# All heads load their projections from pair results; plain gate blocks and the up-projections run as filler beside the attention

## The chip, the core and the metric

The kernel runs on one NeuronCore of one Trainium2 chip. The metric is the device time of one execution in microseconds. Engines: TensorE (PE) with its weight loads (PEld), VectorE (DVE), ScalarE (ACT), GpSimd (POOL), SyncE (SP, here the queue that issues most DMAs).

## What is computed

One layer of a streaming encoder for 512 prompt tokens and 8 x 16 sample tokens, 640 columns in all, D_MODEL 2048. One combined projection feeds three attention branches and three merge gates:

```
parts = rms_norm(x, g_pre) @ w_in      # 6 stick heads q,k,v,g | 6 band heads q,k,v,g | 4 memory heads q,g | 3 gates of 2048
o_sb  = stick_breaking(q, k, v)        # strictly causal, sigmoids and a running product
o_bd  = band_attention(q, k, v, bias)  # softmax over own chunk and the 8 before
o_mm  = memory_attention(q, mk, mv)    # softmax over 256 memory tokens
branch(o, g, w) = (o * silu(g)) @ w
merged = sigmoid(mg_sb) * branch(o_sb, sg, w_up_sb) + sigmoid(mg_bd) * branch(o_bd, bg, w_up_band) \
       + sigmoid(mg_mm) * branch(o_mm, mg, w_up_mem)
y = x + rms_norm(merged @ w_out, g_post)
```

The 128 sample rows attend to caches of 512 rows (256 for memory) for each of 8 streams. Keys and values of the new tokens are outputs too. All is float32.

## The kernel before, in words

A float32 product is made of three matmuls of rounded parts: `split` casts a source to `hi` on ACT and subtracts on DVE for `lo`; then hi x hi, hi x lo, lo x hi. Tokens stand in columns, 640 in two halves of 320. A block is 128 output columns of the combined projection: 16 row tiles x 3 x 2 halves = 96 matmuls. Weights come by SP in half blocks (`wr`, 3 buffers) and are split into `wh` and `wl`. There are 56 head blocks (24 for stick heads, 24 for band heads, 8 for memory heads) and 48 gate blocks.

The stages, in order of the trace:

- Memory keys and values, normalised `x`, and four plain gate blocks (`gate`, `x_proj`): to 137 us.
- Pairs (`block_pair`): two blocks at once with seven half-size products in place of eight, 168 matmuls. 12 pairs make all blocks of the band heads, whose raw results go to DRAM by POOL (`put_raw` into `raw_d`); 22 pairs make the other 44 gate blocks, whose sigmoids go to DRAM by ACT's queue (`put_gate` into `sig_d`). Beside them SP cuts the caches' keys into `keys_d`. To 975 us.
- Attention, 16 heads in the order of `ORDER` (0 to 5 stick, 6 to 11 band, 12 to 15 memory). Band heads load their four raw results (`loaded`, `head_g`); stick heads make their four blocks here and memory heads two, as plain blocks (`transposed`, `head_g`: L383, L393, L394). `head_g` drains its accumulator with a sigmoid on ACT and a multiplication on DVE into an `sg` tile of the pool `stg`, three buffers, which a head holds until its output is written to `osg_d`. A head has three generators: the prompt's attention (11 steps, 9 for memory heads), the samples' score (11 steps) and the samples' output (3 steps); `interleave` goes round them, with the output of the head before.
- Up-projections (`up`): three branches x 16 blocks. `load_o` reads `osg_d` and splits it into `oh` and `ol`; each block is multiplied by a gate from `sig_d` and added into `merged`. These tiles lie where `x` lay, so they wait for the last projection of `x`. To 1858 us.
- The output projection, norm and residual.

Accumulators for projections (`acc`) have two buffers of two PSUM banks; the attention shares four single banks. The program is written in the order of the code, but a planner orders each engine's queue when it is built, by dependencies and its own idea of durations. `tc.issue_after(ins)` binds it: what the block traces on the engine of `ins` comes after `ins` in that queue; it is no wait for its end. Before, only projections are bound so, each behind the one before (`last_mm`); the attention's matmuls stand wherever the planner puts them.

Of the kernel before, what the change touches and what calls it, by code (L numbers as in the profile page):

```python
# [36 lines left out]

FIRST = 4


ORDER = (0, 6, 1, 7, 12, 2, 8, 3, 9, 13, 4, 5, 14, 15, 10, 11)
# [5 lines left out]
def stream_step_kernel(  # L47
# [47 lines left out]
    raw_d = [[dpool.tile([P, NT], F32, name=f"raw_d{n}_{h}") for h in range(6)] for n in range(4)]  # L95
# [92 lines left out]

    def x_proj(col, acc):
# [181 lines left out]
    def loaded(n, h):  # L371
        t = pa.tile([P, NT], F32, tag=f"l{n}", name=f"l{n}", bufs=2 if n == 0 else 1)
# [3 lines left out]
    def transposed(col, n, raw):  # L376

        if raw is not None:
            return loaded(n, raw)
        acc = new_acc()  # L380
        x_proj(col, acc)
        t = pa.tile([P, NT], F32, tag=f"l{n}", name=f"l{n}", bufs=2 if n == 0 else 1)
        ACT.copy(halves(t), acc[:, :, :HF])  # L383
        return t

    def head_g(col, raw=None):
        sg = stg.tile([P, NT], F32, tag="sig", name="sg")
        if raw is not None:
            SP.dma_start(sg, raw_d[3][raw])
            return sg  # L390
        acc = new_acc()
        x_proj(col, acc)
        ACT.activation(halves(sg), acc[:, :, :HF], AF.Sigmoid)  # L393
        DVE.tensor_tensor(halves(sg), acc[:, :, :HF], halves(sg), op=ALU.mult)  # L394
        return sg
# [205 lines left out]
    def causal_head(i):  # L601

        kind, h, c0 = ("sb", i, C_SB) if i < 6 else ("bd", i - 6, C_BD)
# [15 lines left out]
        raw = h if kind == "bd" else None  # L619
        sg = head_g(c0 + 2304 + h * P, raw)  # L620
        vt = transposed(c0 + 1536 + h * P, 2, raw)
# [7 lines left out]
        qt = transposed(c0 + h * P, 0, raw)  # L629
        kt = transposed(c0 + 768 + h * P, 1, raw)  # L630
# [19 lines left out]
    def mem_head(h):  # L650
# [4 lines left out]
        qt = transposed(C_MM + h * P, 0, None)  # L655
        sg = head_g(C_MM + 512 + h * P)
# [26 lines left out]
    def gate(i):  # L683
        acc = new_acc()
        x_proj(C_GATE + i * P, acc)
# [29 lines left out]
    for i in range(FIRST):  # L715
        gate(i)
# [110 lines left out]
    pairs = [(C_BD + 768 * n + h * P, put_raw(n, h)) for n in range(4) for h in range(0, 6, 2)]  # L827
    pairs += [(C_GATE + i * P, put_gate(i)) for i in range(FIRST, 3 * KB, 2)]
# [10 lines left out]
    back = True  # L839
    with tc.tile_pool(name="att", bufs=1, reuse_waits="tile") as pa:  # L840
        qm, wTm = zero_padded(4)

        rest = iter(())
# [4 lines left out]
        interleave(rest)  # L848
    xs.close()

    br = ExitStack()
    pm = br.enter_context(tc.tile_pool(name="mraw", bufs=1, side="right", reuse_waits="tile"))
    merged = pm.tile([P, KB, NT], F32, name="merged")
    po = br.enter_context(tc.tile_pool(name="osgp", bufs=6, side="right", reuse_waits="tile"))
    branches = ((w_up_sb, 6, 0, 0), (w_up_mem, 4, 12, 2 * KB), (w_up_band, 6, 6, KB))
    parts, mark = {}, None

    def load_o(i):
        r = po.tile([P, NT], F32, tag="sig", name="or", bufs=5)
        SP.dma_start(r, osg_d[i])  # L860
        hh = po.tile([P, NT], F32R, tag="oh", name="oh")
        ll = po.tile([P, NT], F32R, tag="ol", name="ol")
        split(hh, ll, r)
        return hh, ll

    def o_src(k):
        return [[t[:, j * HF:(j + 1) * HF] for j in range(2)] for t in parts[k]]

    def up(i):
        nonlocal mark  # L870
        w_up, nh, i0, g0 = branches[i // KB]
        j = i % KB
        if j == 0:
            for h in range(nh):
                parts[h] = load_o(i0 + h)
                if i == 0:
                    mark = last_on(SP)
        acc = new_acc()
        with tc.issue_after(mark if i > 1 else last_mm):
            proj(w_up[0], j * P, nh, o_src, acc)  # L880
        sig = po.tile([P, NT], F32, tag="sig", name="sig", bufs=5)
        with tc.issue_after(mark):
            SP.dma_start(sig, sig_d[g0 + j])
        if i < KB:
            DVE.tensor_tensor(halves(merged[:, j]), acc[:, :, :HF], halves(sig), op=ALU.mult)
        else:
# [115 lines left out]
```

## Time and profile before

| | us |
|---|---|
| median of 3 runs (2084.43 to 2088.02) | 2087.05 |
| the profiled execution | 2088.03 |
| its span, first to last instruction | 2086.3 |
| PE busy | 2045.1 (98%) |
| DVE / ACT / POOL busy | 1104.4 / 817.0 / 570.1 |
| mean granted TensorE clock | 0.994 of 2.4 GHz |

The busy time of PE is made of matmuls whose ends are modelled, so a stretch can be busy and still not at its best pace; the pace is read from the starts. An idle engine costs only where the end of the program hangs on it. A line such as L115 is that of a helper (`split`) with many callers, so groups are told by their tiles.

### The profile page before, as it was taken

How to read it: one execution, taken by the hardware profiler on the slowest of the kernel's cores; microseconds unless marked ns; L12 is line 12 of the kernel's file. 1: busy time of each engine (PE TensorE's matmuls, PEld its weight loads, DVE VectorE, ACT ScalarE, POOL GpSimd, SP SyncE). 2: the span in 40 equal slices, each digit the busy share in tenths (PEclk: the TensorE clock that was granted, in tenths of full speed). 3: DMA queues.
4: the chain of work that ended last, by engine and by line, in shares of the span. 5: the costliest groups of instructions: out<-in, count | busy, mean ns of one | idle time of the engine just before them, and what ended most of it. 6: DMA issues, size and time to landing. Idle time of an engine off the chain costs nothing.

```text
span 2086.3 us, 35971 instructions
## 1 busy us (share of the span) xinstructions
PE 2045.1 (98%) x13997; PEld 1934.7 (93%) x13997; DVE 1104.4 (53%) x1804; ACT 817.0 (39%) x1567; POOL 570.1 (27%) x539
## 2 busy tenths in 40 slices
PE   7999999999999999999999999989999999999998
PEld 5999999999999999999999799979998899998886
DVE  6875555555555555555355645555455665542234
ACT  6543444444444444444233333333334232322221
POOL 1155455664444444441010101010100015330000
PEclk9999999999999999999999999989999999999999
DMA  7656665565556655645557646653556875532225
GB/s 264 213 145 157 166 162 146 140 154 147 147 138 162 164 140 136 154 127 167 154 157 214 186 131 197 195 177 109 164 156 216 242 205 172 166 124 72 81 89 214
DMA packets 556889, 336.49 MB, mean 161 GB/s; under 512 B 271761, under 2 KB 507297, under 8 KB 555181
## 3 DMA queue, kind: packets, MB, share of 16 engines
q1 hardware_dynamic: 542942, 294.53, 50.9%
q0 software_dynamic: 6864, 23.93, 3.3%
q10 hardware_dynamic: 6912, 15.73, 2.0%
q8 instruction: 110, 1.80, 0.4%
q14 instruction: 61, 0.50, 0.1%
HBM read 288.75 MB, written 76.35 MB: 175 GB/s over the span
## 4 chain that ended last, share of the span: by engine, by line
PE 91%; DMA 2%; issue 2%; DVE 2%; POOL 1%; ACT 1%; SPq 0%; DVEq 0%; POOLq 0%; ACTq 0%
PE q L748 40%; PE acc L186 32%; PE ya L171 4%; PE ya L172 3%; PE ya L173 3%; PE s L528 2%; POOL merged L888 1%; PE o L587 1%; DMA kc<-keys_d 1%; DMA wr<-in_w_mem_kv_dram 1%; PE tp L458 1%; PE o L171 1%; DMA or<-osg_d 0%; PE o L172 0%; PE o L173 0%
## 5 line engine op out<-in xcount | busy, mean ns | idle before, releaser
L115 DVE TENSOR_TENSOR wl<-wr,wh 128x512 fp32r<-128x512 f32 (+1 forms) x524 | 383.0, 734 | 384.0 <-ACT wh L114 373.3
L114 ACT CAST wh<-wr 128x512 fp32r<-128x512 f32 (+1 forms) x524 | 316.7, 608 | 607.4 <-PE acc L186 250.5
L115 DVE TENSOR_TENSOR wl<-ws,wh 128x512 fp32r<-128x512 f32 x272 | 231.3, 852 | 232.4 <-ACT wh L114 231.8
L748 PE MATMUL q<-xh,wh 128*128 128x320 f32 x1088 | 336.2, 309 | 0.0
L748 PE MATMUL q<-xh,wl 128*128 128x320 f32 x1088 | 336.2, 309 | 0.0
L748 PE MATMUL q<-xl,wh 128*128 128x320 f32 x1088 | 336.1, 309 | 0.0
L114 ACT CAST wh<-ws 128x512 fp32r<-128x512 f32 x272 | 168.9, 622 | 271.3 <-PE q L748 230.3
L186 PE MATMUL acc<-xh,wl 128*128 128x320 f32 x1152 | 269.9, 312 | 0.0
L186 PE MATMUL acc<-xh,wh 128*128 128x320 f32 x1152 | 267.5, 311 | 1.2 <-DVE sg L394 1.2
L186 PE MATMUL acc<-xl,wh 128*128 128x320 f32 x1152 | 267.7, 311 | 0.0
L748 PE MATMUL q<-th,wl 128*128 128x320 f32 x816 | 252.2, 309 | 0.0
L748 PE MATMUL q<-th,wh 128*128 128x320 f32 x816 | 252.1, 309 | 0.0
L748 PE MATMUL q<-tl,wh 128*128 128x320 f32 x816 | 252.1, 309 | 0.0
L748 PEld LDWEIGHTS q<-xh,wl 128*128 128x128 f32 x1088 | 204.6, 188 | 0.0
L748 PEld LDWEIGHTS q<-xl,wh 128*128 128x128 f32 x1088 | 204.5, 188 | 0.0
L748 PEld LDWEIGHTS q<-xh,wh 128*128 128x128 f32 x1088 | 204.5, 188 | 0.0
L186 PEld LDWEIGHTS acc<-xh,wh 128*128 128x128 f32 x1152 | 193.2, 188 | 8.1 <-issue 5.4
L186 PEld LDWEIGHTS acc<-xl,wh 128*128 128x128 f32 x1152 | 193.5, 188 | 7.6 <-issue 7.5
L186 PEld LDWEIGHTS acc<-xh,wl 128*128 128x128 f32 x1152 | 193.9, 188 | 2.3 <-issue 1.8
L741 POOL TENSOR_TENSOR ws<-wr 128x512 f32<-128x512 f32 x102 | 150.7, 1491 | 93.7 <-DVE wl L115 77.1
L748 PEld LDWEIGHTS q<-th,wl 128*128 128x128 f32 x816 | 153.2, 188 | 0.2 <-DVE wl L115 0.2
L748 PEld LDWEIGHTS q<-tl,wh 128*128 128x128 f32 x816 | 153.2, 188 | 0.0
(239 smaller groups left out, 3262.2 us busy)
## 6 DMA issues: line engine op xcount, KB each, us to landing
wr<-in_w_in_dram SPq DMA_DIRECT2D x208, 512.0 KB, 4.7
kc<-keys_d SPq DMA_DIRECT2D x48, 512.0 KB, 5.0
wr<-in_w_out_dram SPq DMA_DIRECT2D x32, 512.0 KB, 3.7
sig_d<-sig ACTq DMA_DIRECT2D x48, 320.0 KB, 5.3
sig<-sig_d SPq DMA_DIRECT2D x48, 320.0 KB, 3.7
keys_d<-in_cache_sb_k_dram SPq DMA_DIRECT2D x96, 128.0 KB, 4.5
keys_d<-in_cache_band_k_dram SPq DMA_DIRECT2D x96, 128.0 KB, 4.5
vc<-in_cache_sb_v_dram SPq DMA_DIRECT2D x48, 256.0 KB, 5.5
```

Source lines behind the costliest of these rows:

```text
L114: ACT.copy(hi, src)
L115: DVE.tensor_tensor(lo, src, hi.bitcast(F32), op=ALU.subtract)
L171: PE.matmul(out, ah, bh, start=start, stop=False)
L172: PE.matmul(out, ah, bl, start=False, stop=False)
L173: PE.matmul(out, al, bh, start=False, stop=stop)
L186: PE.matmul(acc[:, s, :HF], a[:, k], b[s], start=first and f, stop=last and l)
L458: PE.transpose(tp[:, kb * P:(kb + 1) * P], b[:, kb * P:(kb + 1) * P], ident)
L528: return PE.matmul(s[32 * j:32 * j + 32, :nc_], qm[:, j, par * 32:par * 32 + 32], kts[j], start=par == 0, stop=par == 1, tile_position=(0, ...
L587: PE.matmul(o[32 * j:32 * j + 32, :P], l, r, start=i == 0, stop=i == len(steps) - 1, tile_position=(0, 32 * j))
L741: eng.tensor_tensor(o, a[c], b[c], op=op)
L748: PE.matmul(bank_, a[:, k], b[:, k], start=first and k == 0 and n == 0, stop=k == KH - 1 and n == 2, skip_group_check=not first)
L888: POOL.tensor_tensor(merged[:, j], merged[:, j], sig, op=ALU.add)
```

## The change

- All 16 heads load raw results: the pairs now make the blocks of band, stick and memory heads (12 + 12 + 4 pairs) and 12 gate blocks (6 pairs). `raw_d` gets rows for 16 heads.
- The 32 other gate blocks become plain blocks in the attention, as a generator that stops after each quarter block of 24 matmuls (`proj_steps`, `x_proj_steps`, `gate_steps`).
- Behind the gates the same generator goes on with the up-projections (`up_steps`); a branch waits until its heads' outputs are traced (`done`).
- The loop over heads takes one step of the filler at a head's beginning and 6/8 of a step after each round of the three generators. Everything that the attention traces on PE is bound behind the last filler matmul; the filler is bound behind its own last matmul alone.
- `ORDER` changes; `l0` has one buffer in place of two, `sg` is a tile of the attention's pool with two buffers, `or`/`sig` of the up-projections have four in place of five.

The diff, cut to its core:

```diff
+BESIDE = 32
+PACE = 6
-ORDER = (0, 6, 1, 7, 12, 2, 8, 3, 9, 13, 4, 5, 14, 15, 10, 11)
+ORDER = (0, 6, 1, 12, 2, 7, 3, 13, 4, 8, 5, 14, 9, 15, 10, 11)
...
-    def proj(w, col, kn, src, acc, half=8, back=False):
+    def proj_steps(w, col, kn, src, acc, half=8, back=False):
...
+                if k % 4 == 3 or k == n - 1:
+                    yield
...
+    def x_proj_steps(col, acc):
         nonlocal last_mm, back
-        with tc.issue_after(last_mm or last_on(PE)):
-            proj(w_in, col, KB, x_src, acc, back=back)
-        last_mm, back = last_on(PE), False
+        steps, back = proj_steps(w_in, col, KB, x_src, acc, 8, back), False
+        for _ in range(KB // 4):
+            with tc.issue_after(last_mm or last_on(PE)):
+                next(steps)
+            last_mm = last_on(PE)
+            yield
...
     def loaded(n, h):
-        t = pa.tile([P, NT], F32, tag=f"l{n}", name=f"l{n}", bufs=2 if n == 0 else 1)
+        t = pa.tile([P, NT], F32, tag=f"l{n}", name=f"l{n}")
         SP.dma_start(t, raw_d[n][h])
         return t
...
+    def head_g(h):
+        sg = pa.tile([P, NT], F32, tag="sg", name="sg", bufs=2)
+        SP.dma_start(sg, raw_d[3][h])
         return sg
...
-    def gate(i):
+    def gate_steps(i):
         acc = new_acc()
-        x_proj(C_GATE + i * P, acc)
+        yield from x_proj_steps(C_GATE + i * P, acc)
         sig = stg.tile([P, NT], F32, tag="sig", name="sig")
         ACT.activation(halves(sig), acc[:, :, :HF], AF.Sigmoid)
         put_sig(i, sig)
...
-    pairs = [(C_BD + 768 * n + h * P, put_raw(n, h)) for n in range(4) for h in range(0, 6, 2)]
-    pairs += [(C_GATE + i * P, put_gate(i)) for i in range(FIRST, 3 * KB, 2)]
+    gates = [*range(KB), *range(2 * KB, 3 * KB), *range(KB, 2 * KB)]
+    pairs = [(c + 768 * n + h * P, put_raw(n, i + h)) for c, i in ((C_BD, 6), (C_SB, 0)) for n in range(4) for h in range(0, 6, 2)]
+    pairs += [(C_MM + 512 * n + h * P, put_raw(3 * n, 12 + h)) for n in range(2) for h in range(0, 4, 2)]
+    pairs += [(C_GATE + i * P, put_gate(i)) for i in gates[FIRST:-BESIDE:2]]
...
+    def fill_steps(done):
+        for i in gates[-BESIDE:]:
+            yield from gate_steps(i)
+        xs.close()
...
+        for n, (w_up, nh, i0, g0) in enumerate(branches):
+            while not done.issuperset(range(i0, i0 + nh)):
+                yield
+            parts = [load_o(i0 + h) for h in range(nh)]
...
+            for j in range(KB):
+                yield from up_steps(w_up, nh, o_src, j, n, merged[:, j], g0, po)
...
+    def up_steps(w_up, nh, src, j, n, m, g0, po):
+        nonlocal last_mm
+        acc = new_acc()
+        steps = proj_steps(w_up[0], j * P, nh, src, acc)
+        for _ in range((nh + 3) // 4):
+            with tc.issue_after(last_mm):
+                next(steps)
+            last_mm = last_on(PE)
+            yield
+        sig = po.tile([P, NT], F32, tag="sig", name="sig", bufs=4)
+        SP.dma_start(sig, sig_d[g0 + j])
...
-        for h in ORDER:
-            prompt, score, out = causal_head(h) if h < 12 else mem_head(h - 12)
-            interleave(rest, prompt, score)
+        for n, h in enumerate(ORDER):
+            with tc.issue_after(last_mm or last_on(PE)):
+                prompt, score, out = causal_head(h) if h < 12 else mem_head(h - 12)
+            fill()
+            parts_, due = [rest, prompt, score], 0
+            while parts_:
+                for g in list(parts_):
+                    with tc.issue_after(last_mm or last_on(PE)):
+                        if next(g, parts_) is parts_:
+                            parts_.remove(g)
+                            if g is rest and n:
+                                done.add(ORDER[n - 1])
+                due += PACE
+                fill(due // 8)
+                due %= 8
             rest = out
...
+        for _ in rest:
+            pass
+        done.add(ORDER[-1])
+        for _ in filler:
+            pass
```

## Rows read from the trace of the kernel before

**Rows 1.** The page: busy us (share of the span) and instructions of each engine

```profile
PE 2045.1 (98%) x13997; PEld 1934.7 (93%) x13997; DVE 1104.4 (53%) x1804; ACT 817.0 (39%) x1567; POOL 570.1 (27%) x539
```

**Rows 2.** Stretches: length, busy time per engine (instructions), granted clock, DMA share, GB/s

```profile
137.00:433.00 296.00, 296.00 (x2020) 296.00 (x2019) 158.66 (x205) 123.62 (x223) 168.24 (x127) 1.00 0.60 154
433.00:975.00 542.00, 542.00 (x3696) 541.78 (x3695) 292.70 (x378) 249.79 (x445) 250.30 (x176) 1.00 0.56 144
975.00:1858.00 883.00, 862.10 (x6626) 808.30 (x6624) 474.81 (x905) 309.01 (x652) 115.39 (x195) 0.99 0.60 178
```

**Rows 3.** The chain that ended last, longest pieces: start us, us, what

```profile
80.34 56.32 PE acc L186 x384
136.66 837.98 PE q L748 x5712
974.64 32.12 PE acc L186 x219
...
1592.57 7.27 DMA or<-osg_d
```

**Rows 4.** Short stretches in which PE is not busy, columns as in rows 2

```profile
1177.00:1197.00 20.00, 14.80 (x154) 12.95 (x143) 12.69 (x29) 9.25 (x18) 0.90 (x3) 1.00 0.96 277
1384.00:1411.00 27.00, 18.45 (x153) 14.36 (x152) 17.55 (x39) 9.43 (x17) 2.90 (x7) 0.75 0.70 214
1588.00:1622.00 34.00, 28.40 (x210) 25.55 (x209) 23.52 (x56) 17.19 (x36) 1.63 (x3) 0.95 0.96 304
1403.00:1410.00 7.00, 6.43 (x29) 6.32 (x28) 3.93 (x9) 4.35 (x6) 0.41 (x2) 0.51 0.68 238
```

**Rows 5.** PE in order of time, 1384 to 1412 us: start, us, instruction [idle before]

```profile
1387.86 0.63 PE L568 MATMUL tp<-ident,b 128*128 128x128 f32 x4 [2.01 <-DVE b L473]
...
1396.11 1.02 PE L528 MATMUL s<-kt,qm 128*32 128x256 f32 x8 [2.35 <-DVE sm L482]
...
1402.60 0.52 PE L458 MATMUL tp<-ident,b 128*128 128x128 f32 x3 [3.25 <-DVE b L483]
...
1407.05 0.73 PE L186 MATMUL acc<-xh,wh 128*128 128x320 f32 x2
```

**Rows 6.** All engines in order of time, 1398 to 1408 us

```profile
1399.01 0.54 POOL L596 DMA_DIRECT2D osg_d<-sg  x1 [10.77 <-DVE sg L595]
...
1403.65 1.28 ACT L393 ACT_TABLE_LOAD   x1
...
1405.19 0.70 ACT L393 ACTIVATE sg<-acc 128x640 f32<-128x640 f32 x1 [0.26 <-DMA osg_d<-sg]
...
1405.91 1.28 ACT L481 ACT_TABLE_LOAD   x1
1405.93 0.82 DVE L394 TENSOR_TENSOR sg<-acc,sg 128x640 f32<-128x640 f32 x1 [1.71 <-ACT sg L393]
```

**Rows 7.** PE and ACT in order of time, at the first and third place

```profile
1182.53 0.66 PE L458 MATMUL tp<-ident,b 128*128 128x128 f32 x4 [1.90 <-DVE b L483]
...
1193.86 1.28 ACT L393 ACT_TABLE_LOAD   x1
...
1590.98 0.50 PE L171 MATMUL o<-wth,vh 128*128 128x512 f32 x1 [1.54 <-ACT wth L114]
...
1600.64 0.86 PE L186 MATMUL acc<-oh,wh 128*128 128x320 f32 x4 [1.14 <-ACT oh L114]
```

**Rows 8.** ACT by line, 975 to 1858 us: count | busy us, mean ns | idle before

```profile
L383 ACT COPY l<-acc 128x640 f32<-128x640 f32 x22 | 15.2, 690 | 0.3 <-PE acc L186 0.3
...
L481 ACT ACT_TABLE_LOAD x8 | 10.3, 1283 | 9.1 <-DVE sm L478 9.0
...
L393 ACT ACT_TABLE_LOAD x4 | 5.1, 1283 | 0.1
...
L445 ACT ACT_TABLE_LOAD x3 | 3.8, 1283 | 0.1
```

**Rows 9.** DMA issues: count, KB each, median us to landing

```profile
l<-raw_d SPq DMA_DIRECT2D x18, 320.0 KB, 4.2
```

More of the change, by code (lines that the diff above doesn't have):

```diff
@@ L93, in stream_step_kernel @@
     b12_d = dpool.tile([P, KH, HF], F32, name="b12_d")
-    raw_d = [[dpool.tile([P, NT], F32, name=f"raw_d{n}_{h}") for h in range(6)] for n in range(4)]
+    raw_d = [[dpool.tile([P, NT], F32, name=f"raw_d{n}_{h}") if n in (0, 3) or h < 12 else None for h in range(16)]
+             for n in range(4)]
     sig_d = [dpool.tile([P, NT], F32, name=f"sig_d{i}") for i in range(3 * KB)]
@@ L601, in causal_head @@
     def causal_head(i):
-        kind, h, c0 = ("sb", i, C_SB) if i < 6 else ("bd", i - 6, C_BD)
+        kind, h = ("sb", i) if i < 6 else ("bd", i - 6)
         cv = (cache_sb_v, cache_band_v)[i // 6]
@@ L618, in causal_head @@
             strips = (st[:, TS:], st2)
-        raw = h if kind == "bd" else None
-        sg = head_g(c0 + 2304 + h * P, raw)
-        vt = transposed(c0 + 1536 + h * P, 2, raw)
+        sg = head_g(i)
+        vt = loaded(2, i)
         nat = pa.tile([P, 4, P], F32, tag="nat", name="nat")
@@ L628, in causal_head @@
         vn = natural_new(vt, vs, "vn")
-        qt = transposed(c0 + h * P, 0, raw)
-        kt = transposed(c0 + 768 + h * P, 1, raw)
+        qt, kt = loaded(0, i), loaded(1, i)
         v = split_v(nat)
@@ L715, in stream_step_kernel @@
     for i in range(FIRST):
-        gate(i)
+        for _ in gate_steps(i):
+            pass
         third.append(sums(2 * i))
@@ L839, in stream_step_kernel, with load_o, o_src @@
     back = True
+    br = ExitStack()
+    branches = ((w_up_sb, 6, 0, 0), (w_up_mem, 4, 12, 2 * KB), (w_up_band, 6, 6, KB))
+    def fill_steps(done):
+        for i in gates[-BESIDE:]:
+            yield from gate_steps(i)
+        xs.close()
+        pm = br.enter_context(tc.tile_pool(name="mraw", bufs=1, side="right", reuse_waits="tile"))
+        merged = pm.tile([P, KB, NT], F32, name="merged")
+        po = br.enter_context(tc.tile_pool(name="osgp", bufs=6, side="right", reuse_waits="tile"))
+        def load_o(i):
+            r = po.tile([P, NT], F32, tag="sig", name="or", bufs=4)
+            SP.dma_start(r, osg_d[i])
+            hh = po.tile([P, NT], F32R, tag="oh", name="oh")
+            ll = po.tile([P, NT], F32R, tag="ol", name="ol")
+            split(hh, ll, r)
+            return hh, ll
+        for n, (w_up, nh, i0, g0) in enumerate(branches):
+            while not done.issuperset(range(i0, i0 + nh)):
+                yield
+            parts = [load_o(i0 + h) for h in range(nh)]
+            def o_src(k):
+                return [[t[:, j * HF:(j + 1) * HF] for j in range(2)] for t in parts[k]]
+            for j in range(KB):
+                yield from up_steps(w_up, nh, o_src, j, n, merged[:, j], g0, po)
+        up_done.append(merged)
@@ new lines, in up_steps @@
+    def up_steps(w_up, nh, src, j, n, m, g0, po):
[9 more added lines that the diff above has]
+        SP.dma_start(sig, sig_d[g0 + j])
+        if n == 0:
+            DVE.tensor_tensor(halves(m), acc[:, :, :HF], halves(sig), op=ALU.mult)
+        else:
+            DVE.tensor_tensor(halves(sig), acc[:, :, :HF], halves(sig), op=ALU.mult)
+            POOL.tensor_tensor(m, m, sig, op=ALU.add)
@@ L854, in stream_step_kernel @@
[L854 to L886, printed above, removed]
-            DVE.tensor_tensor(halves(sig), acc[:, :, :HF], halves(sig), op=ALU.mult)
-            POOL.tensor_tensor(merged[:, j], merged[:, j], sig, op=ALU.add)
@@ L890, in stream_step_kernel, with fill @@
-    for i in range(3 * KB):
-        up(i)
+        rest, done = iter(()), set()
+        filler = fill_steps(done)
+        def fill(n=1):
+            for _ in range(n):
+                next(filler, None)
+        for n, h in enumerate(ORDER):
[13 more added lines that the diff above has]
+                due %= 8
+            rest = out
@@ L893, in stream_step_kernel @@
+        for _ in rest:
+            pass
+        done.add(ORDER[-1])
+        for _ in filler:
+            pass
+    merged = up_done[0]
     gparts = [None] * KB
```

30 lines of the change are left out of this document (4 added, 26 removed).

## The prediction

> **What bounds the kernel now.** I read the page's busy line first, then busy time by stretch, then the chain that ended last, then the few stretches in which TensorE (PE) is not busy. PE is busy 98% of the span [rows 1]. From 137 to 975 us, the paired blocks, it is busy in every microsecond; from 975 to 1858 us, the attention and the up-projections, it is busy 862.10 of 883 us [rows 2]. The chain gives the pace: 5712 matmuls of 320 columns in 837.98 us are 0.1467 us each, and the four plain gate blocks, 384 matmuls in 56.32 us, have the same pace [rows 3]. So PE's queue sets the end, and all that can be won without removing matmuls is the 20.9 us of the attention stretch in which it isn't busy, and what a low clock costs there. Nearly all of that lies in three places: of 20, 27 and 34 us PE is busy 14.80, 18.45 and 28.40, so 5.2 + 8.55 + 5.6 = 19.35 us are lost [rows 4]. The second place has also a granted clock of 0.75; its worst seven microseconds stand at 0.51, the 1.2 GHz level, with PE busy nearly throughout, which costs 7 x 0.49 = 3.4 us more [rows 4].
>
> The Trainium skill ("Perfetto Trace Analysis", Identifying the Most-Contended Engine) says that matmul busy time is a poor measure of the distance to the limit and that weight-load busy time is a better one. By it the ceiling would be 883 - 808.30 = 74.7 us [rows 2]; the attention's small matmuls load narrow weights, so I keep to 20.9 and the clock.
>
> Why the second place stands still: PE waits 2.01, 2.35 and 3.25 us for VectorE (DVE), and no projection matmul runs between 1384 and 1407.05 us [rows 5]. The next projection was ready but had no PSUM: its predecessor in the accumulators, a gate block of a head (L393, L394), could be drained only into an `sg` tile, and that came free when an earlier head's output write, issued at 1399.01, had landed; ACT starts L393 at 1405.19 on that DMA, DVE L394 follows at 1405.93, then PE [rows 6]. The first place shows the same drain, behind a table load at 1193.86; its other loss is 1.90 us before `tp`, which waits for a softmax [rows 7].
>
> **The change part by part.** *TensorE's work* stays. Pairs: 12 band, 12 stick, 4 memory and 6 of gates, 34 as before (12 and 22), each 168 matmuls, together the 5712 of [rows 3]. Plain blocks: 4 + 32 as before, only they are gates now and not the stick and memory heads'. The 1536 matmuls of the up-projections stay. Term: 0.
>
> *The paired stage* has 28 pairs that leave raw results (more work for POOL) where it had 12. All 12 of before lie in 137 to 433 us, where PE is busy 296.00 of 296 us, just as with gates behind them [rows 2]. Term 0; the cover is PE's 24.65 us (168 x 0.1467) for each pair, and if the extra POOL work went past it, it would come off one for one.
>
> *The second place* goes. A filler quarter block (24 matmuls, 3.5 us) stands between the attention's steps in 8 of 11 rounds, and a gate block is drained by one ACT sigmoid into a `stg` tile that waits for no head's output. What is late next is the softmax itself, as in the first place. Of 8.55 + 3.4 us nearly all goes: -12 (0 if the waits for DVE come back elsewhere; -15.3 with all of the clock, 27 x 0.25 = 6.75, in place of 3.4).
>
> *The first place* loses its drain; the 1.90 us of softmax stay: 5.2 - 1.9, -3 (-5.2 to 0).
>
> *The third place* is the step from the last `x` block to the first up-projection, whose `oh`/`ol` tiles lie where `x` lay. It exists in both kernels. Before, the attention could pass the waiting up-projection; now each attention step is traced behind the last filler matmul and holds for it. The `or` loads take 7.27 us on the chain [rows 3], and at 1600.64 PE still waits 1.14 us for an `oh` [rows 7]. If nothing covers the load, 7.27 come on top of the 5.6 us; if steps traced earlier cover it, nothing: +3 (-5.6 to +7.3), nearer to the lower end, as four heads' loads overlap each other.
>
> The Trainium skill ("TensorE: Matmul & The Clock Gate", Step-by-step: what each phase is for) says that matmuls stay in program order and only weight loads are pulled ahead: a filler without its operand holds all attention behind it. The trace agrees: PE waits 1.14 us for `oh` and runs nothing else [rows 7]. That speaks against a fixed pace, and is the +3.
>
> *Activation tables.* A gate's sigmoid now falls between the exponentials of band and memory heads. Count: each head makes 1 + floor(11 x 6/8) = 9 fills, a gate's sigmoid comes with every fourth, and the places of those heads in the order (1, 3, 5, 7, 9, 11 to 14) take 18 of the 32. A sigmoid among exponentials needs two table loads of 1.283 us; the stretch had 15 of all kinds, 4 of them for L393 [rows 8], and would get about 36 more, 46 us of ACT. What reaches PE: of the loads for L393, one held the drain at 1193.86 and one held a cast for which PE waited 1.54 us; the exponential's load after it ran ahead [rows 6, 7]. Nothing (the accumulators have two buffers, a fill lies behind most exponentials) to 18 x (1.28 + 0.70), a load and a sigmoid each [rows 6], 36 us. I take +4, some 0.2 us each, as the quarter block behind is 3.5 us and the load 1.28.
>
> By the Trainium skill ("ScalarE: Activation LUTs", What ACT_TABLE_LOAD costs) a switch is 1283 ns of load and about 1380 ns of drain, 2.66 us; the 36 would then be 96 us of ACT. The trace has the 1283 [rows 8], but L393 starts 1.54 us after its load began, 0.26 of that idle [rows 6]: no drain is seen.
>
> *The loads.* SP issues 32 more loads of raw results (56 against 24, 4.2 us to landing); the 22 copies of L383 (0.69 us of ACT each) and L394's multiplications go, and ACT's queue gets 32 `sig_d` writes in this stretch [rows 8, 9]. `l0` has one buffer where it had two, `sg` has two; behind a load that waits for a buffer SP holds `kc` and weight loads. None of PE's waits of [rows 5, 7] ends on such a load. 0, up to 10 heads x 4.2 = 42 if each new head waited for one.
>
> Sum: 2086.3 - 12 - 3 + 3 + 4 = 2078.3 us of span. The median of the runs, 2087.05, stands 0.75 above that span (the profiled execution itself took 2088.03), so **2079 us**.
>
> **The rivals.** *Covered throughout:* tables and loads are all hidden, and the third place too: 2086.3 - 20.9 - 3.4 + 0.75 = 2062.8. For it: the paired stage runs without any gap. Against: the third place has the same memory reuse.
>
> *No change:* the idle time belongs to the softmax chains, which PE's order meets anywhere: 2083 to 2091, with 2087 in the middle. For it: the three long waits of [rows 5] end on DVE, none on a missing weight.
>
> *Slower by the tables:* ACT runs in order, so each of 18 sigmoids delays a split or a softmax by its load. It decides from (12 + 3 - 3)/18 = 0.67 us each; at 1.283 us the sum is 2086.3 - 12 - 3 + 3 + 23 + 0.75 = 2098, with the sigmoid's 0.70 as well 2111. For it: both cases of [rows 7]. Against: PE then had no filler between.
>
> *The pace doesn't hold:* fills are tied to each other only, so the planner may run them ahead of the attention. The gates (128 of 144 fills) then end early, the up-projections can't begin before the last stick head is done, and each head left bare costs what the second place cost, 12 us. Two heads: 2079 + 24 = 2103. For it: before, the attention stretch opens with 219 projection matmuls in a row [rows 3]. Against: attention steps can't run ahead of their fills, so fills run ahead only where a step is late.
>
> **How the numbers follow.** Forecast (2070 to 2083) 0.46; covered throughout 0.13; no change 0.20; tables 0.14; pace 0.07. About 0.2% of the time, 4.2 us, can be told from no change: faster is below 2082.9, slower above 2091.2. Faster 0.59, same 0.20, slower 0.21. The range leaves out some of the covered case and the far ends of the last two: 2062 to 2101.
>
> **What would show it.** PE busy in the stretch after the pairs should rise from 862 of 883 to at least 870; no hole of the kind at 1384 to 1407; the granted clock at its 2.4 GHz level but for the step to the up-projections; some 50 table loads where 15 were; POOL's, not PE's, row growing in the paired stage. Wrong: PE waiting for a `wth` cast or a softmax behind a gate's sigmoid, a stretch of attention without filler before the first up-projection, or PE waiting for a raw load at a head's beginning.

## The result and the profile after

The changed kernel takes 2066.28 us in the median (2065.98 to 2067.31), the kernel before 2087.39 on the same chip: a ratio of 0.9902 (0.9885 to 0.9920). The forecast was 2079.0 in a range of 2062 to 2101: faster, as forecast, but by 21 us where 8 were worked out.

The page of the changed kernel, busy time of each engine, then the granted clock in 40 equal slices of the span (9 is 90% or more of 2.4 GHz); [rows 1] has the first line for the kernel before:

```profile
PE 2038.2 (99%) x13997; PEld 1929.4 (93%) x13997; DVE 1099.2 (53%) x1794; ACT 842.1 (41%) x1575; POOL 613.1 (30%) x581
...
PEclk9999999999999999999999999999999999999999
```

PE's matmuls are as many as before. The mean granted clock over the span is 0.997 where it was 0.994: worked out from these means, 6.2 of 2065.6 us are lost to the low clock level, where 12.5 of 2086.3 were.

Stretches of the changed kernel, columns as in [rows 2, 4]: the paired stage; attention and up-projections; the attention up to the last block of `x`; the step to the up-projections; and the first and second places of [rows 4]:

```profile
137.00:975.00 838.00, 837.54 (x5709) 837.06 (x5709) 456.15 (x580) 358.31 (x642) 461.92 (x346) 1.00 0.58 148
975.00:1838.00 863.00, 857.22 (x6648) 806.29 (x6648) 463.77 (x897) 349.35 (x684) 117.07 (x196) 1.00 0.69 207
978.00:1577.00 599.00, 599.00 (x4765) 556.36 (x4763) 321.45 (x654) 265.67 (x522) 54.46 (x146) 1.00 0.72 217
1577.00:1611.00 34.00, 30.27 (x225) 25.89 (x224) 27.01 (x53) 17.54 (x36) 3.11 (x8) 1.00 0.98 301
...
1384.00:1411.00 27.00, 27.00 (x242) 25.76 (x231) 14.70 (x32) 10.89 (x21) 0.90 (x3) 1.00 0.79 248
1177.00:1197.00 20.00, 20.00 (x145) 19.99 (x144) 11.41 (x23) 8.04 (x20) 2.72 (x9) 1.00 0.69 211
```

For 599 us PE is busy in every microsecond. Of 20.9 us without a matmul between the pairs and the output projection 5.8 are left, 3.73 of them in the step to the up-projections. In the profile of a2_after, the same kernel once more, that step has the same busy time but a clock of 0.95, so the 1.00 above is that of one execution:

```profile
1577.00:1611.00 34.00, 30.26 (x215) 25.34 (x215) 25.51 (x49) 16.91 (x35) 3.12 (x8) 0.95 0.97 303
```

From the first matmul behind the pairs to the first of the output projection the kernel before took 884.29 us (974.47 to 1858.76), the changed one 860.31 (977.89 to 1838.20): -24.0. The stages ahead of the pairs took 2.7 us more in this execution (the pairs began between 134.9 and 139.7 us in the executions of all kernels below, changed or not), the paired stage 0.7 and the rest 0.1 less; together -20.7 us of span.

PE's remaining waits in the attention and the up-projections of the changed kernel, by what ended them (us in total, times, longest), then PE in order of time in the step to the up-projections:

```profile
PE acc L189 <- DVE ol L118: 2.8, 3, 1.3
PE tp L565 <- ACT vn L410: 1.3, 1, 1.3
PE acc L189 <- ACT oh L117: 1.1, 2, 0.7
PE tp L455 <- DVE b L480: 0.6, 1, 0.6
```

```profile
1581.26 0.44 PE L565 MATMUL tp<-ident,e 128*128 128x128 f32 x2 [1.27 <-ACT vn L410]
...
1582.23 0.46 PE L189 MATMUL acc<-oh,wh 128*128 128x320 f32 x2
...
1587.73 0.63 PE L455 MATMUL tp<-ident,b 128*128 128x128 f32 x4 [0.59 <-DVE b L480]
...
1589.66 0.56 PE L189 MATMUL acc<-oh,wh 128*128 128x320 f32 x2 [0.66 <-ACT oh L117]
1591.43 0.56 PE L189 MATMUL acc<-ol,wh 128*128 128x320 f32 x2 [1.22 <-DVE ol L118]
```

Where the softmax (`b`) held PE longest before [rows 5, 7], one wait of 0.6 us is left. What remains are mostly the first operands of the up-projections (`oh`, `ol`).

### The profile page after: what moved, and what is told of

It reads as the page before. It is cut to its first block, busy times and chain, and to the rows that moved or that the text cites. A ratio compares the mean times of both kernels' runs of the same rounds, so it can differ in the third digit from the quotient of the medians.

```text
span 2065.6 us, 36060 instructions
## 1 busy us (share of the span) xinstructions
PE 2038.2 (99%) x13997; PEld 1929.4 (93%) x13997; DVE 1099.2 (53%) x1794; ACT 842.1 (41%) x1575; POOL 613.1 (30%) x581
## 4 chain that ended last, share of the span: by engine, by line
PE 91%; issue 2%; POOL 2%; DMA 2%; DVE 1%; ACT 1%; SPq 0%; DVEq 0%; ACTq 0%; POOLq 0%
PE q L743 39%; PE acc L189 33%; PE ya L174 4%; PE ya L176 4%; PE ya L175 4%; PE s L525 2%; PE o L584 1%; POOL merged L885 1%; PE tp L455 1%; DMA raw_d<-sl 1%; POOL ws L736 1%; PE o L175 0%; PE s L174 0%; PE o L176 0%; PE o L174 0%
## 5 line engine op out<-in xcount | busy, mean ns | idle before, releaser
L118 DVE TENSOR_TENSOR wl<-ws,wh 128x512 fp32r<-128x512 f32 x272 | 236.6, 873 | 229.9 <-ACT wh L117 229.4
L736 POOL TENSOR_TENSOR ws<-wr 128x512 f32<-128x512 f32 x102 | 155.2, 1535 | 82.2 <-DVE wl L118 68.2
L743 PEld LDWEIGHTS q<-th,wh 128*128 128x128 f32 x816 | 153.2, 188 | 0.7 <-ACT sig L760 0.7
```

Source lines behind the costliest of these rows:

```text
L118: DVE.tensor_tensor(lo, src, hi.bitcast(F32), op=ALU.subtract)
L736: eng.tensor_tensor(o, a[c], b[c], op=op)
L743: PE.matmul(bank_, a[:, k], b[:, k], start=first and k == 0 and n == 0, stop=k == KH - 1 and n == 2, skip_group_check=not first)
```

## The experiments

The first theory was that of the prediction: the gain is the gate blocks' release from the heads' buffers, the tie that [rows 6] show (a head's gate drains into an `sg` that waits for an earlier head's output write). The rivals: TensorE's order, bound by quarter blocks; the order of heads; and, later, how the filler is shared out over the heads and within them. Ratios are to the kernel before on the same chip, with the 95% interval; one thousandth is 2.1 us.

| kernel | median us | ratio |
|---|---|---|
| changed kernel, again (a2_after) | 2065.98 | 0.9907 (0.9894 to 0.9921) |
| e1_unbound | 2064.73 | 0.9896 (0.9877 to 0.9914) |
| e5_oldorder | 2066.20 | 0.9903 (0.9886 to 0.9919) |
| e8_before_up4 | 2089.69 | 1.0016 (1.0008 to 1.0025) |
| e7_before_sg5_up4 | 2079.49 | 0.9964 (0.9951 to 0.9977) |
| e6_before_sg5 | 2126.57 | 1.0192 (1.0175 to 1.0209) |
| e3_pace10 | 2163.58 | 1.0368 (1.0352 to 1.0384) |
| e9_pace10_unbound | 2166.42 | 1.0383 (1.0369 to 1.0397) |
| e4_pace3 | 2071.28 | 0.9926 (0.9914 to 0.9939) |
| e11_pace7 | 2069.01 | 0.9920 (0.9908 to 0.9932) |
| e12_lumped | 2085.71 | 0.9992 (0.9983 to 1.0001) |
| e14_even_lump | 2073.70 | 0.9940 (0.9928 to 0.9953) |
| e15_uneven_spread | 2081.07 | 0.9977 (0.9968 to 0.9986) |
| e16_tied | 2067.49 | 0.9911 (0.9897 to 0.9925) |
| e2_copygate | 2063.04 | 0.9893 (0.9875 to 0.9910) |
| e10_more_tables | 2074.42 | 0.9942 (0.9930 to 0.9955) |
| e13_late_sigmoid | 2070.93 | 0.9918 (0.9906 to 0.9931) |

**The binding and the order of heads.** e1_unbound takes the `issue_after` off the attention's steps; e5_oldorder has the kernel before's order; a2_after is the changed kernel once more.

```diff
-            with tc.issue_after(last_mm or last_on(PE)):
-                prompt, score, out = causal_head(h) if h < 12 else mem_head(h - 12)
+            prompt, score, out = causal_head(h) if h < 12 else mem_head(h - 12)
...
-                    with tc.issue_after(last_mm or last_on(PE)):
-                        if next(g, parts_) is parts_:
+                    if next(g, parts_) is parts_:
```

> The changed kernel, but the attention's TensorE instructions are no longer bound behind the last filler matmul; the planner may put them anywhere. Theory 'cover' (the binding puts 3.5 us of filler behind nearly every attention step, and that hides softmax and drains): holes come back, PE not busy for more than 12 us of the attention stretch where the changed kernel has 5.8, time 2073 to 2085 us. Rival 'drain' (the gain is only that no head's output tile holds an accumulator any more): still 2064 to 2069 us, PE not busy for 4 to 8 us.

```diff
-ORDER = (0, 6, 1, 12, 2, 7, 3, 13, 4, 8, 5, 14, 9, 15, 10, 11)
+ORDER = (0, 6, 1, 7, 12, 2, 8, 3, 9, 13, 4, 5, 14, 15, 10, 11)
```

> The changed kernel with the order of heads of the kernel before. Theory 'cover' (it is the filler, not which head follows which): 2063 to 2070 us. Rival 'order' (the gain comes from having stick and softmax heads alternate, so that no two softmax heads follow each other early): 2074 to 2087 us, with holes where two softmax heads follow each other.

> The changed kernel again, on the chip of the next three, as their base: 2063 to 2069 us.

All three lie within one another's intervals. In e1 PE is without a matmul for 5.4 us of 863, so it meets the numbers of 'drain' and not of 'cover'; e12 and e16 below show that the drain is not the reason. The planner puts the filler in nearly the same places without the binding: ahead of the samples' scores at 1202 and 1546 us of the changed kernel 1186 and 2928 filler matmuls are counted in the trace, ahead of the same scores of e1 1187 and 2936. So the order by quarter blocks, as far as it is a matter of `issue_after`, has no part in the time. It lies in the order in which the code emits the blocks, as e12 to e15 show.

**The tie.** In the kernel before, `sg` is taken by turns from a tile of the attention's pool and from `stg`, and `l0` gives up a buffer for the space (e6). e7 has four buffers of `or` and `sig` besides, as the changed kernel has; e8 has only that.

```diff
-        sg = stg.tile([P, NT], F32, tag="sig", name="sg")
+        nonlocal heads
+        heads += 1
+        sg = pa.tile([P, NT], F32, tag="sg", name="sg", bufs=2) if heads % 2 else stg.tile([P, NT], F32, tag="sig", name="sg")
...
-        r = po.tile([P, NT], F32, tag="sig", name="or", bufs=5)
+        r = po.tile([P, NT], F32, tag="sig", name="or", bufs=4)
```

> The kernel before with sg tiles taken in turn from two pools, five buffers in place of three (and l0 with one buffer), all else as before. Rival 'drain': the accumulator no longer waits for a head's output write, the hole at 1384 to 1407 us goes and most of the first: 2071 to 2076 us. Theory 'cover': the drain is one of several waits that a step without filler behind it meets; the hole shrinks or moves, 2079 to 2088 us.

> The kernel before with five sg buffers as in e6_before_sg5, and the up-projections' or and sig tiles with four buffers in place of five, so that they fit where x lay and do not wait for the attention's memory as they did in e6. Rival 'drain': without the wait of a projection's accumulator for a head's output write the kernel before gives up its first two holes: 2064 to 2074 us. Theory 'cover' as revised (a filler must be traced beside every head, with or without the binding): holes stay, 2079 to 2086 us.

> The kernel before with the up-projections' or and sig tiles at four buffers in place of five and nothing else: the control for e7_before_sg5_up4. 'Drain' and 'cover': 2082 to 2088 us, the holes at 1177, 1384 and 1588 us as before. If the fifth buffer itself held the up-projections back: below 2080 us, with the hole at 1588 us gone.

Stretches of e6, then of e7, columns as above:

```profile
973.00:1573.00 600.00, 593.36 (x4683) 552.54 (x4682) 316.72 (x624) 214.88 (x467) 52.86 (x143) 1.00 0.60 172
1573.00:1666.00 93.00, 53.93 (x413) 36.49 (x412) 50.80 (x124) 28.02 (x71) 8.79 (x22) 0.71 0.55 159
```

```profile
975.00:1577.00 602.00, 595.12 (x4695) 553.84 (x4696) 317.16 (x625) 216.07 (x470) 52.97 (x143) 1.00 0.61 173
1577.00:1611.00 34.00, 25.46 (x185) 21.13 (x185) 24.56 (x58) 16.39 (x35) 1.63 (x3) 0.90 0.93 302
```

In both the second place's hole is gone: 6.6 and 6.9 us without a matmul are left in 600, spread over the heads. But e6 is slower by 40 us: the larger pool seems to lie over the space of the up-projections' tiles (e7, which shrinks them, starts its first up-projection at 1581.39 us). In e6 the first one starts at 1665.8 us, after the last head's output write at 1662.62, and from the last `x` block at 1573.5 on the heads run bare, PE busy 53.93 of 93 us at a clock of 0.71. e7, which moves those tiles back, gains 7.5 us on the kernel before and 11 on its control e8 (which came out 1.7 us above the range expected). Both ranges for e6 missed; 2079.49 for e7 lies in that of 'cover'. So the tie costs 8 to 11 us in the kernel before, where the second buffer of `l0` was given up too; 13 us lie between e7 and the changed kernel.

**The pace.** PACE is 6 eighths of a quarter block each round; e4 has 3, e11 7, e3 10, and e9 is e3 without the binding.

```diff
-PACE = 6
+PACE = 10
```

> The changed kernel with PACE 3: 1 + floor(33/8) = 5 fills a head, 17.6 us of filler traced beside each, the rest after the attention. The fillers are bound only to each other, so the planner may take them early. If a quarter block must be traced behind each step ('cover' by order): more waits of TensorE on softmax and casts, 2072 to 2090 us. If what counts is only that some filler is ready whenever the attention is not: 2063 to 2069 us.

> The changed kernel with PACE 7: 1 + floor(77/8) = 10 fills a head, the gates end with the thirteenth head, when the last stick head is done, so no head is left bare and the up-projections begin one head earlier. 'Supply' (what counts is that some filler is ready at all times): 2063 to 2070 us. If the step from the last x block to the first up-projection is what is left to win: 2060 to 2064 us, as more heads lie beside it.

> The changed kernel with PACE 10: 1 + floor(110/8) = 14 fills a head, so the 128 gate fills are traced by the tenth head and the up-projections cannot begin before the last stick head's output, one or two heads later. The prediction's rival 'the pace doesn't hold' prices a head without filler at 12 us: 2078 to 2092 us, with bare attention before the first up-projection and a lower granted clock there. If the planner spreads the fillers whatever the trace order: 2063 to 2069 us.

> PACE 10 as in e3_pace10, with the attention not bound behind the filler as in e1_unbound. It parts the 97 us that PACE 10 cost into attention without filler (12 us a head, two to three heads: 24 to 36 us, so 2090 to 2102 us here) and attention held behind an up-projection that waits for its heads (the rest). If the binding is no part of it: 2155 to 2170 us again.

Stretches of e3, where PE has no filler:

```profile
1530.00:1610.00 80.00, 45.88 (x403) 34.45 (x401) 43.70 (x93) 31.54 (x67) 8.67 (x23) 0.77 0.69 210
1700.00:1850.00 150.00, 114.79 (x866) 102.37 (x858) 88.75 (x163) 39.34 (x90) 36.29 (x38) 0.86 0.62 186
```

At 10 the 32 gate blocks are used up at 1531 us, and the filler is a queue: gates, stick branch, memory branch, band branch, each of which waits for its last head. In between some five heads have nothing beside them (an estimate from the stretches without a filler matmul), and the kernel is 97 us slower than the changed one, some 19 us a head. Their clock falls with PE's idle time: 0.77 where PE is busy 45.88 of 80 us, 1.00 where it is busy throughout. The Trainium skill ("TensorE: Matmul & The Clock Gate", What's actually happening) says that the gate follows how busy the engine is; these rows agree in the large. e3 is far above the 2092 that I had as its upper end. e9 is as slow, so the binding is no part of it. At 7 and 3 the kernel is 3 to 5 us slower than at 6: the best pace is broad, and its far side is steep.

The near side is flat because the planner takes filler forward. In e4 only 80 of the 128 quarter blocks of gates are traced beside the heads, the others behind the last one. Yet its last gate matmul starts at 1581.82 us (1577.34 in the changed kernel), and its last head writes its output at 1689.71. So filler that is traced too late is drawn to where it is needed. The time of e4, 2071.28, lies between its two theories.

**How the filler is shared out.** e12 is e1 with the kernel before's order and its share: 16 quarter blocks emitted ahead of each stick head, 8 ahead of each memory head, none for band heads, none by rounds. e14 keeps the changed kernel's order and even share, 9 for each head, but emits them at the head's start. e15, again with the order of before, emits by rounds, but only beside stick and memory heads. None of the three binds the attention, and none ties a filler block to a head. By the code e12 and e15 trace 128 and 122 steps of filler beside the heads, where e14 and the changed kernel trace 144, the last 16 of them up-projections; e4, with 80, shows that this alone costs some 5 us at most.

```diff
-            fill()
+            fill(16 if h < 6 else 8 if h > 11 else 0)
...
-                due += PACE
-                fill(due // 8)
-                due %= 8
```

That is e12; e14 has `fill(9)` in that place, and e15 this:

```diff
-            fill()
+            pace = 11 if h < 6 else 6 if h > 11 else 0
...
-                due += PACE
+                due += pace
```

> The changed kernel without its order of quarter blocks, with the kernel before's order of heads and its lumped share of filler: 16 quarter blocks emitted ahead of each stick head, 8 ahead of each memory head, none ahead of a band head, none by rounds. The fillers still belong to no head's buffers. Theory 'untied': that the fillers wait for no head is what counts, so 2064 to 2070 us. Rival 'even share': that each head, the band heads too, has filler of its own beside it is what counts, so 2075 to 2084 us, with holes round the band heads' first blocks.

> The changed kernel without its order of quarter blocks and its own order of heads, with the same 9 quarter blocks for each head as it has, but all 9 emitted at the head's beginning and none by rounds. Theory 'even over the heads': each head has its share, and the order in which PE's queue takes them inside a head is of no importance: 2064 to 2072 us. Rival 'spread inside the head': 2077 to 2088 us, with waits of PE for the softmax in the second half of each head.

> The kernel before's order of heads, no order of quarter blocks, and filler by rounds only beside stick heads (11/8 of a quarter block each round) and memory heads (6/8), none beside band heads. Theory 'even over the heads': the bare band heads cost what they cost in e12_lumped, 2077 to 2088 us, with holes round band heads. Rival 'spread inside the head': as fast as the changed kernel, 2064 to 2072 us.

The same stretches of e12 as of the changed kernel above, then of e14 (975 to 1572 and on) and e15 (1200 to 1400, and 34 us at its step to the up-projections):

```profile
978.00:1577.00 599.00, 592.78 (x4658) 550.10 (x4657) 306.15 (x597) 237.76 (x476) 52.27 (x143) 1.00 0.70 206
1577.00:1611.00 34.00, 28.97 (x214) 26.76 (x214) 22.63 (x56) 17.28 (x38) 1.24 (x4) 0.90 0.86 286
```

```profile
975.00:1572.00 597.00, 595.28 (x4668) 552.48 (x4667) 311.10 (x621) 252.07 (x498) 53.37 (x143) 1.00 0.72 212
1572.00:1606.00 34.00, 28.62 (x242) 27.32 (x244) 21.41 (x52) 17.32 (x36) 1.51 (x3) 0.90 0.84 260
```

```profile
1200.00:1400.00 200.00, 196.96 (x1613) 183.03 (x1612) 108.56 (x212) 88.16 (x169) 19.86 (x55) 1.00 0.75 217
...
1579.00:1613.00 34.00, 25.93 (x169) 18.88 (x169) 26.65 (x54) 16.43 (x33) 3.15 (x8) 0.90 0.95 292
```

e12 gives the whole gain back: 2085.71, 19 us behind the changed kernel (0.9992 less 0.9902), though nothing in it is tied to a head. 'Even share' is upheld, past the upper end that I gave it; its holes, though, are not where I expected them. The chain of e12 (start us, us, what) shows where the filler goes; that of before opens much alike, with 219 filler matmuls in a row [rows 3]; the changed kernel's follows as the second fence:

```profile
977.93 7.04 PE acc L189 x48
984.97 0.44 PE t L621 x4
985.51 2.21 PE acc L189 x15
987.83 47.08 PE acc L189 x321
```

```profile
978.06 7.04 PE acc L189 x48
985.10 0.44 PE t L621 x4
985.64 2.21 PE acc L189 x15
987.96 1.32 PE acc L189 x9
989.28 0.23 PE s L174
989.52 1.03 PE acc L189 x7
```

Some 380 filler matmuls, 56 us of cover, go by in e12 before the first score at 1034.91. The changed kernel goes over to the first scores after 72. So the heads of e12 come late: the first output write is issued at 1089.28 us and the last at 1743.92, where the changed kernel has 1042.81 and 1677.06 (the kernel before 1095.02 and 1739.98). e12's waits of PE between the pairs and the output projection (us in total, times, longest):

```profile
PE acc L189 <- ACT oh L117: 4.7, 2, 4.0
PE tp L494 <- ACT oh L117: 4.6, 1, 4.6
PE o L175 <- DVE wtl L118: 4.3, 2, 2.5
PE tp L455 <- DVE b L480: 1.9, 2, 1.0
```

The two longest stand at the up-projections, not in the middle of the attention. At 1585.07 PE waits 4.6 us; the profile puts that down to an `oh`, but the matmul reads the `b` of a softmax, whose exponential starts at 1583.78 behind the sigmoid of the last gate block and two table loads (1580.10 and 1582.48). At 1706.28 it waits 4.0 us for an `oh` of the memory branch, one of two whose loads are issued from 1698.85 us on. About half of what e12 loses to the changed kernel is lost behind 1570 us: 11 us without a matmul against 6, with the clock at 0.96 to 0.98 against 0.98 to 1.00. That the share of the filler is the cause is shown by the time; how the loss parts into late heads, waits and clock is read from this one execution.

Changed one at a time, emitting at the head's start costs 8 us (e14, between its two theories; 5.2 of them stand in one place, below), and leaving the band heads without filler costs 16 (e15); both at once, 19. The profiled execution of e15 was the fastest of its eleven (2074.20 us against a median of 2081.07), so its rows show less than it costs: 3.0 us without a matmul in the 200 and 8.1 in the 34, with a clock of 0.90.

PE in order of time in e14, at its step to the up-projections:

```profile
1572.98 0.46 PE L189 MATMUL acc<-xh,wl 128*128 128x320 f32 x2
1578.67 1.12 PE L565 MATMUL tp<-ident,e 128*128 128x128 f32 x4 [5.24 <-DVE e L480]
```

With all nine quarter blocks of the head emitted at its start, none is left when this softmax is late. And it is late behind the sigmoid of the last gate block, with a table load on either side (ACT in e14):

```profile
1573.60 1.28 ACT L681 ACT_TABLE_LOAD   x1
...
1575.62 1.28 ACT L478 ACT_TABLE_LOAD   x1
1576.91 0.83 ACT L478 ACTIVATE e<-e,sm 128x640 f32<-128x640 f32 x1
```

That left e7's gain to explain: untying helped the kernel before, but e12, untied, is no faster than it. e16 puts the tie back into the changed kernel, as far as it goes: `sg` and the gates' drains share three buffers again, but a head's gate is loaded there and not drained.

```diff
-        sg = pa.tile([P, NT], F32, tag="sg", name="sg", bufs=2)
+        sg = stg.tile([P, NT], F32, tag="sig", name="sg")
```

> The changed kernel with the tie put back: a head's `sg` comes from the pool `stg` of three buffers again, out of which the filler's gate blocks are drained. Theory 'the tie costs by itself': 2073 to 2077 us, 7 to 10 us more, with PE waiting for a gate's drain behind a head's output write. Rival 'with filler beside every step the drain has slack': 2065 to 2069 us.

The rival is upheld: 2067.49, 1.9 us behind the changed kernel and inside its interval. In 978 to 1577 us PE is without a matmul for 1.5 us:

```profile
978.00:1577.00 599.00, 597.48 (x4756) 555.02 (x4756) 321.10 (x656) 265.76 (x523) 54.84 (x145) 1.00 0.72 216
```

None of its 32 drains beside the heads shows ACT waiting for a head's output write, as L393 did at 1405.19 [rows 6]. So the tie does not hold up the changed kernel, and the share of the filler is the cause of the gain. Why e12, with the tie gone, is no faster than the kernel before, where the tie alone was worth 8 to 11 us, no run tells: e12 with the tie put back was not run.

**The activation tables.** e2 drains the 32 gate blocks beside the attention by a copy; their sigmoid is left out of the computation. e10 adds a tiny exponential and a tiny sigmoid to each of these blocks. e13 drains by a copy too, but applies the sigmoid later, in the up-projections.

```diff
-        ACT.activation(halves(sig), acc[:, :, :HF], AF.Sigmoid)
+        if i < FIRST:
+            ACT.activation(halves(sig), acc[:, :, :HF], AF.Sigmoid)
+        else:
+            ACT.copy(halves(sig), acc[:, :, :HF])
```

e13 has this besides, in `up_steps`:

```diff
+        if n > 0:
+            ACT.activation(sig, sig, AF.Sigmoid)
```

> The changed kernel with the 32 gate blocks beside the attention drained by a copy in place of a sigmoid (these gates lack their sigmoid), so that ACT needs no table load for them: 45 loads in the attention stretch become about 11 to 13. Theory 'cover' (a table load is hidden by the quarter block behind it): 2064 to 2068 us, no change. The prediction's term of 4 us: 2062 us. If each of the 34 loads cost its 1.28 us on TensorE's path: near 2023 us; half of them: 2045 us.

> The changed kernel with two activations of 128 x 1 elements (an exponential, then a sigmoid) behind the second quarter of each of the 32 gate blocks beside the attention, so that the table is switched more often: 95 loads in the attention stretch for 45, 64 us more of ACT. If loads are hidden by the filler: within 3 us of the changed kernel. By the prediction's term (4 us for 34 loads): 6 us more. If each load cost its 1.28 us: 64 us more.

> The changed kernel with the 32 gate blocks beside the attention drained by a plain copy, their sigmoid applied later, in the stage of the up-projections after the attention; the result is the reference's. Some 34 table loads fewer beside the attention. Theory 'loads cost 0.1 to 0.2 us each': 2061 to 2065 us against the changed kernel's 2066 to 2068. Rival 'the added sigmoid on ScalarE and its wait in the up-projections give it back': 2065 to 2070 us.

The changed kernel has 45 table loads in the attention, e2 11, e10 95, e13 12. ACT of the changed kernel in order of time, round two of them:

```profile
1126.61 1.28 ACT L681 ACT_TABLE_LOAD   x1
1127.91 0.70 ACT L681 ACTIVATE sig<-acc 128x640 f32<-128x640 f32 x1
...
1133.05 1.28 ACT L478 ACT_TABLE_LOAD   x1 [1.71 <-DVE sm L477]
1134.34 0.47 ACT L478 ACTIVATE b<-s,sm 128x256 f32<-128x256 f32 x1
```

50 loads more, with the 64 tiny activations that bring them, cost 8.4 us (0.0040), at most 0.17 us a load, and make PE idle again (978 to 1577: 594.60 of 599). 34 fewer make 1.9 us (e2, 0.0009), less than the intervals, and e13, which leaves nothing out, is no faster either (0.9918 against 0.9902). So nothing that the times can show is to be won from the 45 loads: the rows of 978 to 1577 us have no idle time that they could cause. The trace shows one place where they reach PE, the last gate block, behind which only the up-projections are left as filler. Its load and sigmoid stand ahead of the `vn` copy for which PE waits at 1581.26:

```profile
1577.96 1.28 ACT L681 ACT_TABLE_LOAD   x1
1579.26 0.70 ACT L681 ACTIVATE sig<-acc 128x640 f32<-128x640 f32 x1
...
1580.94 0.26 ACT L410 COPY vn<-t 128x128 f32<-128x128 f32 x1
```

In e2 and e13, without that load, PE waits 0.42 us there in place of 1.27, and 0.28 in place of 0.59 for the next softmax: 1.2 us in all.

The Trainium skill ("ScalarE: Activation LUTs", What ACT_TABLE_LOAD costs) adds some 1380 ns of drain to each load of 1283; here the function starts 0.02 us behind the load's end, and no drain shows.

## Why the prediction was right and wrong

**What held.** PE's queue is the bound, its work is unchanged, and the paired stage takes the POOL work for 0.7 us: POOL's row there grew to 461.92 us while PE stayed at 837.54 of 838. The `l` and `sg` loads cost nothing: none of PE's waits above ends on one. Table loads in the attention: some 50 were forecast, 45 came. There is no bare stretch at the pace chosen. The price of one, 12 us a head, was taken from another kind of hole; it is met in e6 (48 us more than e7, four heads) and low in e3 (19 by my estimate).

**The term that was mis-sized most: the third place, +3.** I reasoned that each attention step now holds for a late up-projection. It fell instead: 5.60 us without a matmul became 3.73, and the clock of 0.95 [rows 4] became 1.00, which is 1.7 us more: -3.6. In a2_after the clock stands at 0.95, so these 1.7 us are those of one execution, and -1.9 is what both show. The argument rested on the binding, and e1 shows that the binding moves nothing. PE's row there without it:

```profile
1577.00:1611.00 34.00, 30.83 (x223) 27.33 (x222) 25.85 (x50) 13.64 (x29) 3.17 (x8) 0.95 0.99 304
```

The loss goes with how the filler is shared out: PE is busy 28.97, 28.62 and 25.93 of 34 us in e12, e14 and e15, each at 0.90. I had the bound in hand (-5.6) and took the wrong end. Error: 4.9 to 6.6 us.

**The first place, -3.** I let the 1.90 us of softmax stay, since a softmax would be as late as before. All 5.2 us went (20.00 of 20). A filler quarter block in front of the step covers the softmax, which I had counted on at the second place and not here. Error: 2.2 us.

**The second place, -12.** The 8.55 us went entirely, and so did all of the low clock: 27 x 0.25 = 6.75 us, where I had taken only the seven microseconds at the 1.2 GHz level, 3.4. The far end of my bound, -15.3, was right for this profile. Error: 3.3 us. How the low clock parts over the places is partly chance: e8, which differs from the kernel before by one buffer of `or` and `sig`, has 0.91, 0.87 and 0.85 in the same three places, where [rows 4] have 1.00, 0.75 and 0.95.

**The tables, +4.** No idle time of PE in 978 to 1577 us is left that they could cause; 1.2 us stand behind the last gate's load, in the step to the up-projections. My 0.2 us each is what a load costs beyond the number there (at most 0.17 in e10); the 30 added here came nearly free. Error: some 3 us.

Measured so, the three places give -15.3 - 5.2 - 3.6 = -24.1; waits elsewhere are 0.5 us longer, and near 1755 us a clock of 0.83 over 10 us costs 1.7. That is -21.9 of the -24.0; the other 2 us I cannot place. All four errors have one sign. At the first place and the tables they have one cause: I priced each hole by its own releaser and asked what would be late next there, when the change puts filler beside every step of every head, which covers any releaser. At the second place I left out most of the low clock, and at the third I gave the binding a cost that e1 does not show. The rival 'covered throughout' (2062.8), to which I gave 0.13, was nearer than the forecast: 3.5 us off.

**The mechanism, in part wrong.** For the second place the prediction names two things, the filler between the attention's steps and the release of the gate's drain from the heads' buffers, and reads the hole itself as the work of the tie. That release is worth 8 to 11 us by itself in the kernel before (e7), but it isn't what makes the changed kernel fast: with the tie it loses 1.9 us, which is inside the interval (e16), without the even share it loses 19 (e12). The half that names the filler was right. The reason given for it, a fixed order of filler and steps, was not, since e1 has no such binding.

**The rivals.** 'No change' fails: the softmax waits went. 'Tables' fails at this number of loads, though its mechanism shows at the last gate block, for 1.2 us here and within the 5.24 us of e14. 'Pace doesn't hold' fails as stated: the planner does take fills forward (e4), but not so far that a head stays bare. Its price is real as soon as the code itself uses the gates up early (e3). 'PE busy at least 870 of 883' was a poor sign to look for: the stretch became shorter, and PE's busy time with it (857.22 of 863).

**What stays open.** How much of e14's 8 us is the burst at a head's start and how much its step to the up-projections, where PE stood for 5.24 us behind a softmax, wasn't told apart. Nor was how much of e12's loss comes from its late heads and how much from the clock, and why untying helps the kernel before and not e12.

## What to carry to other kernels

Where one engine sets the end and a chain of small steps beside it has waits, count the independent work that can stand beside each step, and emit it evenly: a share for every head, spread over its steps, not a lump where it happens to be produced. A lump that was emitted early stayed ahead of the head and made it late (e12, 19 us); filler that was emitted late was drawn forward (e4, 5 us). Such cover removed waits whatever ended them, so price it by all idle time of the stretch and the clock that goes with it, not hole by hole. Where the cover ends, at the step to the up-projections here, waits remain. Keep enough of it to the last head: a head left bare cost 12 to 19 us here, half the pace 5.

## What was unexpected of the hardware

A table load costs ACT 1.28 us and what stands behind it starts 0.02 us later; on PE's path it cost at most 0.17 us when 50 were added to 45, and nothing that could be measured when 34 were taken away. Bare heads lose by the clock as well as by waits: in e6 PE has no matmul for 39 of 93 us, and the mean granted clock over them is 0.71. The clock does not follow the program alone. The step to the up-projections stands at 1.00 in one profile of the changed kernel and at 0.95 in another, with PE busy 30.27 and 30.26 of the same 34 us. The same program spread over 2074.20 to 2086.14 us in e15, with a mean granted clock of 0.993 to 0.996; the changed kernel's four runs lie within 1.4 us, those of a2_after within 4.4.
